# Output projection of a gMLP layer by column halves with four blocks' rows kept, and weight sums on VectorE at longer intervals

## The chip, the cores and the metric

The kernel runs on one core of one Trainium2 chip. The metric is device time of one execution in microseconds (us); the median of several runs counts.

## What is computed

A two-layer decoder trunk on a residual stream x of 2048 rows by 1024 columns, in float32. Layer 0 is a hybrid attention layer (eight heads of dilated sliding-window attention and four heads of differential attention behind one input projection). Layer 1, which is the last stage of the kernel, is a gated MLP:

```python
h = rms_norm(x, norm_g)
u, v, g = split(h @ w_in)                     # 1024 -> 3 x 2048
u = gelu(u)
v = layer_norm(gelu(v), ln_g, ln_b)
sp = einsum('gts,bnsgc->bntgc', tril(w_s), v by chunks of 128 rows, 8 groups) + b_s
y = u * sp * silu(g)
x = x + y @ w_out                             # 2048 -> 1024
```

## The kernel before

Rows are handled in 16 blocks of 128. TensorE (PE) multiplies in a split float32 form: every operand is held as a rounded high part and a low rest, made by `split` (L91): a cast on ScalarE (L92) and a subtraction on VectorE (L93). A product then takes three matmuls: high by high, high by low, low by high.

The order of PE's instructions is the order of the program. The other engines' orders, and those of the DMA queues, come from a planner that simulates the kernel; each queue is then in order. Most loads are issued from the SP queue, most stores from the POOL queue. A tile belongs to a tag with a fixed number of buffers, and a new tile waits for the release of the oldest.

Stage one (0 to about 1420 us) runs eight units. In each, `project` multiplies all 16 blocks by one eighth of the input weights, and between its steps the attention of the unit before is woven in. `quarter_sums` (L282) is woven in too: in 48 pieces it loads parts of the last layer's input weights (L290), takes four differences on GpSimd (POOL, L292 to L295) and stores them (L296) as tensors `t`; `project` calls it once in every block above 8 (L330). It has one buffer, tag tq. Then come `out_first` and `out_second`, the attention's output projections. `out_second` reloads the first half's sums (L766, SP queue), adds, stores x1, squares its rows (L779) and, but for the last two blocks, scales, transposes and stores them as `h2`.

The last stage (from about 1750 us) takes the blocks in four groups of four. Per group it forms `v`, `u` and `g` by Strassen's scheme (seven products, `strassen` L914) in two column rounds (cc 0 and 1). `rows_sums` (L964) loads h2 and makes the seven row operands; their scaling for the last two blocks is left to `turn` (L997), called in the first group. Weights come through `slot` (L861): either a raw load of 512 KB into one of three wr buffers and a split into one of five w2 buffers, or, where `kept` names a copy made earlier, a load of the 1 MB high and low parts from HBM (tensor `ws`). After `g` of a round comes the output projection (L1145 to L1170): for each of two column sets c, four slots with all 1024 output columns are fetched, and for each of the four blocks the rows of y are transposed and split (`turned`, tag yT2, two buffers) and multiplied, 12 matmuls for each half of the output columns, L1161 to L1163:

```python
seq = [(c, b) for c in range(2) for b in blocks]
...
wo2 += slot(wout[:, k0 + k:k0 + k + 1], 1, k0 + k)
```

The first group splits these weights and stores them; groups two to four load the stored form. So there are eight projections, two per group. The mixing in `u` uses another pair of buffers, tag vs.

Of the kernel before, what the change touches and what calls it, by code (L numbers as in the profile page):

```python
# [8 lines left out]
F32 = mybir.dt.float32  # L9
# [8 lines left out]
P = 128  # L18
# [17 lines left out]
DWR, WS, VS_BUFS = 3, 5, 2  # L36
# [24 lines left out]
def _trunk(tc, a, out):  # L61
# [3 lines left out]
    with ExitStack() as top:  # L65
# [25 lines left out]
        def split(hi, lo, src, E=V):  # L91
            A.copy(hi, src)  # L92
            return E.tensor_sub(lo, src, hi.bitcast(F32))  # L93
# [24 lines left out]
        with ExitStack() as st:  # L118
# [161 lines left out]
            def quarter_sums():  # L280


                for m in (1, 0, 2):
                    for kc in range(4):
                        for e in range(0, 1024, 256):
# [6 lines left out]
                            G.tensor_sub(t[:, 0, 0], t[:, 0, 1], t[:, 0, 0])  # L292
                            G.tensor_sub(t[:, 0, 1], t[:, 1, 1], t[:, 0, 1])
                            G.tensor_sub(t[:, 1, 1], t[:, 1, 1], t[:, 0, 0])
                            G.tensor_sub(t[:, 1, 0], t[:, 1, 0], t[:, 1, 1])  # L295
                            G.dma_start(t_s[m][kc][:, :, e:e + 256], t.rearrange("p a b e -> p (a b) e"))  # L296

# [9 lines left out]
            def project(c):  # L307
# [4 lines left out]
                for b in range(NB):  # L312
# [11 lines left out]
                    for dc in range(DC):  # L324
# [5 lines left out]
                        if not first and b > 8 and dc == 1:  # L330
                            next(sums, None)
# [416 lines left out]
            def out_second():  # L748
# [77 lines left out]
        with ExitStack() as st:  # L826
# [17 lines left out]
            for tag, bufs, shape, dt in (  # L844
# [3 lines left out]
                    [("acc", GB, [P, D], F32), ("ln", 2, [P, 2, 512], F32), ("yT2", 2, H, F32R),  # L848
                     ("vs", VS_BUFS, [P, 2, 512], F32R), ("wsp", 1, [P, 2, SG, P], F32R), ("vn", 2, [P, 512], F32),
# [9 lines left out]
            last_load = None  # L859

            def slot(src, n, kept=None):  # L861


                nonlocal last_load
# [4 lines left out]
                else:  # L869
                    raw = tile_([P, 2, 512], F32, "wr", DWR).rearrange("p k e -> p (k e)").rearrange("p (n e) -> p n e", n=n)  # L870
                    last_load = nc.sync.dma_start(raw, src)
                    split(z[:, 0], z[:, 1], raw)
# [90 lines left out]
            def rows_sums(gi, j):  # L963
# [5 lines left out]
                for k in range(2):  # L969
                    nc.sync.dma_start(hr[:, 2 * k:2 * k + 2].rearrange("p q c t -> p (q c t)"), h2_s[b + 2 * k])  # L970
# [4 lines left out]
                def parts(i, src):  # L975
                    split(ht[i][:, 0], ht[i][:, 1], src)
# [20 lines left out]
            def turn(b):  # L997

                with tc.issue_after(urgent.ins):
                    factor(w1, b)  # L1000
                for n in range(2):
                    xr = tile_([P, 512], F32, "ct", 4)
                    nc.sync.dma_start(xr, x1_s[b][:, 512 * n:512 * n + 512])
                    A.activation(xr, xr, AF.Copy, scale=r2[b][:, 0:1])
                    pt = psum("pp", [P, 512], 2).rearrange("p (c t) -> p c t", t=P)
                    for i in range(4):
                        T.transpose(pt[:, i], xr[:, i * P:i * P + P], ident)
# [13 lines left out]
            for gi in range(NG):  # L1021
# [44 lines left out]
                for cc in range(2):  # L1066
# [61 lines left out]
                    def turned(b, c):  # L1128
# [4 lines left out]
                        yT = tile_(H, F32R, "yT2", 2)  # L1133
# [11 lines left out]
                    seq = [(c, b) for c in range(2) for b in blocks]  # L1145
                    for n, (c, b) in enumerate(seq):
                        if n % GB == 0:
                            k0 = columns(cc, c).start // P
                            wo2 = []
                            for k in range(4):  # L1150
                                wo2 += slot(wout[:, k0 + k:k0 + k + 1], 1, k0 + k)
                        yT, nxt = nxt, turned(seq[n + 1][1], seq[n + 1][0]) if n < 7 else None
                        if cc == 0 and c == 0:
# [3 lines left out]
                        for h in range(2):  # L1157
                            es = slice(512 * h, 512 * h + 512)
                            po = psum("y", [P, 512], 3)
                            for i in range(4):  # L1160
# [69 lines left out]
```

## Time and profile before

| what | us |
|---|---|
| median of 3 runs | 3221.08 |
| lowest and highest | 3219.82, 3221.86 |
| the profiled execution | 3229.59 |
| its span | 3227.8 |
| PE busy in the span | 3021.7 (94%) |
| VectorE busy | 2042.0 (63%) |
| ScalarE busy | 1588.7 (49%) |
| GpSimd busy | 859.9 (27%) |

The span runs from the first to the last instruction that the profiler saw; 1.8 us of the profiled execution lie around it. PE busy overstates PE's work, since matmuls overlap in the records: one of 128x512 is recorded with some 0.39 us, while the next one starts 0.23 us after it. PEclk is TensorE's granted clock; 1.00 stands for 2.4 GHz and 0.50 for 1.2 GHz, and a value between is a mean over a stretch.

### The profile page before, as it was taken

The numbers are of one execution on the slowest core, as the hardware profiler recorded it, in microseconds if no ns is written. First come the engines' busy times: TensorE is split into PE (matmuls) and PEld (weight loads), VectorE is DVE, ScalarE is ACT, GpSimd is POOL, SyncE is SP. The second block draws the span as 40 slices with busy tenths as digits, with TensorE's granted clock in tenths as the row PEclk, the third lists the DMA queues.
The fourth block names the chain that finished last, engine by engine and source line by source line (L and its number), as shares of the span: only waits on it lengthen the run. The fifth ranks groups of instructions, "written<-read, shape, count | busy, mean of one in ns | idle before, by whom it ended". The sixth has DMA issues, their size and how long they took to land.

```text
span 3227.8 us, 45405 instructions
## 1 busy us (share of the span) xinstructions
PE 3021.7 (94%) x15240; PEld 2516.7 (78%) x15240; DVE 2042.0 (63%) x4582; ACT 1588.7 (49%) x2964; POOL 859.9 (27%) x2031
## 2 busy tenths in 40 slices
PE   7889999999999998999998899999899999999998
PEld 6678777887888787887886788787787777777787
DVE  5435775467745685467777686858465774758463
ACT  5535655455555555544455564545252553436251
POOL 5537563565536564552121000000000000000000
PEclk9999999999999999999999999999999999999999
DMA  9977967687687967768347776677465764557553
GB/s 346 333 217 242 257 217 217 218 244 224 204 231 228 266 201 218 244 192 238 126 147 265 248 241 254 223 240 242 156 201 202 250 215 150 177 191 245 182 170 143
DMA packets 376074, 710.68 MB, mean 220 GB/s; under 512 B 62113, under 2 KB 176929, under 8 KB 363553
## 3 DMA queue, kind: packets, MB, share of 16 engines
q1 hardware_dynamic: 348640, 603.70, 59.7%
q0 software_dynamic: 27200, 104.09, 8.5%
q8 instruction: 120, 1.97, 0.3%
q14 instruction: 114, 0.93, 0.1%
HBM read 531.25 MB, written 151.26 MB: 211 GB/s over the span
## 4 chain that ended last, share of the span: by engine, by line
PE 72%; DMA 13%; DVE 8%; ACT 3%; issue 2%; SPq 1%; POOL 0%; ACTq 0%; DVEq 0%; POOLq 0%
PE x L926 15%; PE y L926 11%; PE pm L326 5%; PE pm L327 4%; PE pm L328 4%; PE y L1161 4%; PE y L1162 3%; PE y L1163 3%; PE po L645 3%; PE pu L549 3%; DMA w<-ws 3%; PE s_ps L506 3%; DMA hT<-hts 2%; PE sd_ps L608 2%; PE sd_ps L609 2%
## 5 line engine op out<-in xcount | busy, mean ns | idle before, releaser
L926 PE MATMUL x<-w,h 128*128 128x512 f32 x2304 | 557.2, 396 | 15.0 <-ACT w L92 9.4
L93 DVE TENSOR_TENSOR w<-wr,w 128x1024 fp32r<-128x1024 f32 x328 | 399.3, 1220 | 205.1 <-ACT w L92 203.8
L926 PEld LDWEIGHTS x<-w,h 128*128 128x128 f32 x2304 | 433.4, 190 | 115.1 <-ACT w L92 10.5
L326 PE MATMUL pm<-wh,hT 128*128 128x512 f32 x1024 | 452.5, 442 | 53.0 <-DMA hT<-hts 33.3
L92 ACT CAST w<-wr 128x1024 fp32r<-128x1024 f32 x328 | 341.8, 1048 | 239.4 <-PE y L1163 89.6
L926 PE MATMUL y<-w,h 128*128 128x512 f32 x1728 | 414.0, 393 | 0.0
L327 PE MATMUL pm<-wl,hT 128*128 128x512 f32 x1024 | 409.6, 400 | 2.3 <-POOL wl L93 2.3
L328 PE MATMUL pm<-wh,hT 128*128 128x512 f32 x1024 | 410.1, 401 | 0.1
L926 PEld LDWEIGHTS y<-w,h 128*128 128x128 f32 x1728 | 322.9, 188 | 71.9
L326 PEld LDWEIGHTS pm<-wh,hT 128*128 128x128 f32 x1024 | 199.8, 195 | 76.1 <-issue 19.5
L1161 PE MATMUL y<-w,yT 128*128 128x512 f32 x512 | 219.6, 429 | 39.7 <-DMA w<-ws 39.7
L1164 DVE TENSOR_TENSOR acc<-y,acc 128x512 f32<-128x512 f32 x128 | 88.3, 690 | 236.1 <-PE y L1163 236.1
L328 PEld LDWEIGHTS pm<-wh,hT 128*128 128x128 f32 x1024 | 196.5, 192 | 45.8 <-DVE hT L218 0.9
L615 ACT ACTIVATE sd<-sd,nmd 128x128 f32<-128x128 f32 (+15 forms) x128 | 154.0, 1203 | 135.1 <-DVE nmd L611 130.6
L327 PEld LDWEIGHTS pm<-wl,hT 128*128 128x128 f32 x1024 | 199.4, 195 | 20.6 <-POOL wl L93 4.6
L1163 PE MATMUL y<-w,yT 128*128 128x512 f32 x512 | 210.5, 411 | 3.6 <-DVE yT L93 3.6
L1162 PE MATMUL y<-w,yT 128*128 128x512 f32 x512 | 210.6, 411 | 0.2 <-DVE w L93 0.2
L517 ACT ACTIVATE sm<-sm,um 128x256 f32<-128x256 f32 (+1 forms) x256 | 115.6, 486 | 138.0 <-DVE um L515 137.7
L549 PEld LDWEIGHTS pu<-vt,pTs 128*128 128x128 f32 x1200 | 161.5, 193 | 27.3 <-ACT u L552 9.0
L515 DVE CUSTOM_DVE_ANT_0 sm<-s_ps,masks 128x256 f32<-128x256 f32 (+1 forms) x224 | 84.8, 415 | 142.1 <-PE s_ps L506 142.0
L549 PE MATMUL pu<-vt,pTs 128*128 128x65 f32 x1200 | 157.7, 269 | 11.1 <-ACT u L552 7.2
L1161 PEld LDWEIGHTS y<-w,yT 128*128 128x128 f32 x512 | 101.9, 199 | 73.4 <-DMA w<-ws 52.9
(217 smaller groups left out, 5986.5 us busy)
## 6 DMA issues: line engine op xcount, KB each, us to landing
hT<-hts SPq DMA_DIRECT2D x224, 512.0 KB, 4.8
wr<-t SPq DMA_DIRECT2D x168, 512.0 KB, 4.5
wr<-in_sgu_w_in SPq DMA_DIRECT2D x144, 512.0 KB, 4.6
w<-ws SPq DMA_DIRECT2D x72, 1024.0 KB, 6.9
tq<-in_sgu_w_in SPq DMA_DIRECT2D x96, 256.0 KB, 3.4
t<-tq POOLq DMA_DIRECT2D x48, 512.0 KB, 4.7
ws<-w POOLq DMA_DIRECT2D x24, 1024.0 KB, 8.4
hts<-hT SPq DMA_DIRECT2D x32, 512.0 KB, 7.0
```

The source lines that it names most:

```text
L92: A.copy(hi, src)
L93: return E.tensor_sub(lo, src, hi.bitcast(F32))
L326: T.matmul(pm, z[:, 0, k], w[dc][0], start=dc == 0, stop=False)
L327: T.matmul(pm, z[:, 0, k], w[dc][1], start=False, stop=False)
L328: T.matmul(pm, z[:, 1, k], w[dc][0], start=False, stop=dc == DC - 1)
L517: A.activation(sm[:, t, :w], sm[:, t, :w], AF.Exp, bias=nm, scale=-1.0)
L549: T.matmul(pu[:, g0 % 4 + t], pTs[:, t, P * q:P * q + P], vt[pat][:, vb, 65 * i:65 * i + 65], start=q == 0, stop=q == nk - 1)
L615: A.activation(sm[:, :L], sm[:, :L], AF.Exp, bias=nm[:, nch - 1:nch], scale=-1.0, accum_out=lsum)
L926: T.matmul(acc, z[:, p, kc], w[kc][q], start=start and kc == k == 0, stop=kc == 3 and k == 2, skip_group_check=True)
L1161: T.matmul(po, yT[:, 0, i], wo2[i][0][:, es], start=i == 0, stop=False)
L1162: T.matmul(po, yT[:, 0, i], wo2[i][1][:, es], start=False, stop=False)
L1163: T.matmul(po, yT[:, 1, i], wo2[i][0][:, es], start=False, stop=i == 3)
```

## The change

- The output projection takes, for each column set c, first one half of the output columns for all four blocks and then the other. Its weights come in two slots per half (two weight rows by 512 columns each) instead of four per column set, always raw and split, with no copy kept in HBM. The transposed rows of the four blocks are made in the first half and kept for the second. They now share the tag vs, which has four buffers; yT2 is gone.
- `turn` comes after the seventh and eleventh of sixteen steps (before: after the fourth and sixth of eight), loads both halves first and squares the rows itself; `out_second` no longer squares the last two blocks.
- The first group's h2 loads are issued from ScalarE's queue instead of SP, and its row splits are queued behind the latest weight split on ScalarE and VectorE.
- `out_second` loads x1p from the POOL queue instead of SP.
- The weight sums are subtracted on VectorE. Load and subtraction are separate steps, taken in turn from block 4 of a unit on, two steps per 12 of `project`'s steps.

```diff
-DWR, WS, VS_BUFS = 3, 5, 2
+DWR, WS, VS_BUFS = 3, 5, 4
...
         def split(hi, lo, src, E=V):
-            A.copy(hi, src)
-            return E.tensor_sub(lo, src, hi.bitcast(F32))
+            return A.copy(hi, src), E.tensor_sub(lo, src, hi.bitcast(F32))
...
                             yield
-                            G.tensor_sub(t[:, 0, 0], t[:, 0, 1], t[:, 0, 0])
...
+                            V.tensor_sub(t[:, 0, 0], t[:, 0, 1], t[:, 0, 0])
...
                             G.dma_start(t_s[m][kc][:, :, e:e + 256], t.rearrange("p a b e -> p (a b) e"))
+                            yield
...
-                        if not first and b > 8 and dc == 1:
+                        if not first and b > 3 and (8 * b + dc) % 12 in (8, 3):
                             next(sums, None)
...
-                        nc.sync.dma_start(x1[n], x1p_s[b][:, 512 * n:512 * n + 512])
+                        G.dma_start(x1[n], x1p_s[b][:, 512 * n:512 * n + 512])
...
-                    for n in range(2):
-                        sq = w1.tile([P, 512], F32, name="sqx", tag="wr", bufs=WR_BUFS)
-                        A.activation(sq, x1[n], AF.Square, accum_out=r2[b][:, 2 + n:3 + n])
                     if b < NB - LATE:
+                        for n in range(2):
+                            sq = w1.tile([P, 512], F32, name="sqx", tag="wr", bufs=WR_BUFS)
+                            A.activation(sq, x1[n], AF.Square, accum_out=r2[b][:, 2 + n:3 + n])
                         factor(w1, b)
...
-                    nc.sync.dma_start(hr[:, 2 * k:2 * k + 2].rearrange("p q c t -> p (q c t)"), h2_s[b + 2 * k])
+                    (nc.sync if gi else nc.scalar).dma_start(hr[:, 2 * k:2 * k + 2].rearrange("p q c t -> p (q c t)"), h2_s[b + 2 * k])
...
                 def parts(i, src):
-                    split(ht[i][:, 0], ht[i][:, 1], src)
+                    with ExitStack() as behind:
+                        if gi == 0 and halves:
+                            for z in halves:
+                                behind.enter_context(tc.issue_after(z.ins))
+                        split(ht[i][:, 0], ht[i][:, 1], src)
...
             def turn(b):
-                with tc.issue_after(urgent.ins):
-                    factor(w1, b)
+                xr = [tile_([P, 512], F32, "ct", 4) for _ in range(2)]
                 for n in range(2):
-                    xr = tile_([P, 512], F32, "ct", 4)
-                    nc.sync.dma_start(xr, x1_s[b][:, 512 * n:512 * n + 512])
-                    A.activation(xr, xr, AF.Copy, scale=r2[b][:, 0:1])
+                    nc.sync.dma_start(xr[n], x1_s[b][:, 512 * n:512 * n + 512])
+                    sq = tile_([P, 512], F32, "th", 2)
+                    A.activation(sq, xr[n], AF.Square, accum_out=r2[b][:, 2 + n:3 + n])
+                factor(w1, b)
+                for n in range(2):
+                    A.activation(xr[n], xr[n], AF.Copy, scale=r2[b][:, 0:1])
...
-                        yT = tile_(H, F32R, "yT2", 2)
+                        yT = tile_([P, 2, 512], F32R, "vs", VS_BUFS).rearrange("p k (c t) -> p k c t", t=P)
...
-                    seq = [(c, b) for c in range(2) for b in blocks]
-                    for n, (c, b) in enumerate(seq):
+                    seq = [(c, h, b) for c in range(2) for h in range(2) for b in blocks]
+                    yT = {blocks[0]: nxt}
+                    for n, (c, h, b) in enumerate(seq):
+                        es = slice(512 * h, 512 * h + 512)
                         if n % GB == 0:
                             k0 = columns(cc, c).start // P
                             wo2 = []
-                            for k in range(4):
-                                wo2 += slot(wout[:, k0 + k:k0 + k + 1], 1, k0 + k)
-                        yT, nxt = nxt, turned(seq[n + 1][1], seq[n + 1][0]) if n < 7 else None
-                        if cc == 0 and c == 0:
+                            for k in range(0, 4, 2):
+                                wo2 += slot(wout[:, k0 + k:k0 + k + 2, es], 2)
+                        if n + 1 < len(seq) and seq[n + 1][1] == 0:
+                            yT[seq[n + 1][2]] = turned(seq[n + 1][2], seq[n + 1][0])
+                        if cc == 0 and c == h == 0:
                             acc[b] = tile_([P, D], F32, "acc", GB)
...
-                        for h in range(2):
-                            es = slice(512 * h, 512 * h + 512)
-                            po = psum("y", [P, 512], 3)
...
+                        po = psum("y", [P, 512], 3)
+                        for i in range(4):
+                            T.matmul(po, yT[b][:, 0, i], wo2[i][0], start=i == 0, stop=False)
+                            T.matmul(po, yT[b][:, 0, i], wo2[i][1], start=False, stop=False)
+                            T.matmul(po, yT[b][:, 1, i], wo2[i][0], start=False, stop=i == 3)
...
-                        if gi == 0 and cc == 0 and n in (3, 5):
-                            turn(NB - LATE + n // 4)
-                        for _ in range(2):
-                            next(todo, None)
+                        if gi == 0 and cc == 0 and n in (6, 10):
+                            turn(NB - LATE + n // 8)
+                        next(todo, None)
```

## Rows read from the trace of the kernel before

**Rows 1.** The page's chain that ended last, by engine.

```profile
PE 72%; DMA 13%; DVE 8%; ACT 3%; issue 2%; SPq 1%; POOL 0%; ACTq 0%; DVEq 0%; POOLq 0%
```

**Rows 2.** Eight projections: stretch, us, five engines' busy time, PEclk, DMA, GB/s.

```profile
1930.21:1982.08 51.87, 49.61 (x236) 40.25 (x234) 26.99 (x37) 13.65 (x19) 2.67 (x5) 1.00 0.62 245
2066.25:2119.13 52.88, 48.40 (x220) 38.19 (x218) 35.92 (x53) 16.98 (x26) 2.66 (x5) 1.00 0.72 275
2285.94:2345.42 59.48, 51.39 (x219) 40.18 (x218) 18.35 (x26) 7.28 (x11) 0.00 (x0) 0.94 0.25 99
2429.57:2486.90 57.33, 50.81 (x219) 39.61 (x218) 28.07 (x43) 11.38 (x18) 0.00 (x0) 0.94 0.45 170
2650.50:2711.63 61.13, 53.81 (x219) 41.76 (x218) 18.35 (x26) 7.28 (x11) 0.00 (x0) 0.89 0.25 96
2795.78:2857.32 61.54, 53.68 (x219) 41.73 (x218) 27.98 (x43) 11.39 (x18) 0.00 (x0) 0.89 0.37 141
3022.67:3083.62 60.95, 53.96 (x220) 41.99 (x218) 18.36 (x26) 7.30 (x11) 0.00 (x0) 0.89 0.25 95
3167.77:3223.70 55.93, 50.74 (x219) 39.68 (x217) 16.40 (x24) 4.45 (x8) 0.00 (x0) 0.94 0.32 125
```

**Rows 3.** PE, third projection: start, us, what, [idle before <-releaser].

```profile
2285.94 0.47 PE L1161 MATMUL y<-w,yT 128*128 128x512 f32 x1
...
2289.22 0.50 PE L1161 MATMUL y<-w,yT 128*128 128x512 f32 x1 [1.64 <-DMA w<-ws]
...
2321.53 0.79 PE L1161 MATMUL y<-w,yT 128*128 128x512 f32 x1 [1.55 <-DMA w<-ws]
...
2345.42 1.79 PE L926 MATMUL x<-w,h 128*128 128x512 f32 x7
```

**Rows 4.** The page's groups of instructions, output projection and weight split.

```profile
L1161 PE MATMUL y<-w,yT 128*128 128x512 f32 x512 | 219.6, 429 | 39.7 <-DMA w<-ws 39.7
...
L93 DVE TENSOR_TENSOR w<-wr,w 128x1024 fp32r<-128x1024 f32 x328 | 399.3, 1220 | 205.1 <-ACT w L92 203.8
...
L92 ACT CAST w<-wr 128x1024 fp32r<-128x1024 f32 x328 | 341.8, 1048 | 239.4 <-PE y L1163 89.6
```

**Rows 5.** The chain in order of time: start, us, what (two windows of it).

```profile
2240.88 11.11 PE x L926 x48
...
2295.59 0.44 PE pp L1132 x4
...
2322.33 0.43 PE y L1162
```

**Rows 6.** The page's DMA issues: count, KB, median us to landing.

```profile
wr<-in_sgu_w_in SPq DMA_DIRECT2D x144, 512.0 KB, 4.6
...
w<-ws SPq DMA_DIRECT2D x72, 1024.0 KB, 6.9
```

**Rows 7.** PE in order of time, second projection: its longest wait.

```profile
2076.65 0.63 PE L1132 MATMUL pp<-ident,vv 128*128 128x128 f32 x4 [2.98 <-DVE vv L1126]
```

**Rows 8.** Start of the last stage, in order of time: PE, ScalarE, VectorE.

```profile
1741.01 0.63 ACT L779 ACTIVATE sqx<-x 128x512 f32<-128x512 f32 x1 [2.07 <-DVE x L731]
...
1750.42 0.79 PE L926 MATMUL x<-w,h 128*128 128x512 f32 x1 [9.37 <-ACT w L92]
1753.98 7.35 PE L926 MATMUL x<-w,h 128*128 128x512 f32 x23 [2.77 <-DVE w L93]
...
1744.28 1.29 DVE L93 TENSOR_TENSOR h<-hr,h 128x512 fp32r<-128x512 f32 x2
```

**Rows 9.** Waits (us, times, longest) and one group of lines.

```profile
POOL tq L292 <- DMA tq<-in_sgu_w_in: 105.5, 36, 7.6
...
SPq L290 <- DMA t<-tq: 177.2, 40, 9.2
...
PE pm L326 <- DMA hT<-hts: 10.8, 7, 4.6
...
L509 DVE TENSOR_TENSOR sm<-s_ps,masks 128x256 f32<-128x256 f32 x80 | 33.8, 423 | 103.6 <-PE s_ps L506 103.4
```

More of the change, by code (lines that the diff above doesn't have):

```diff
@@ L291, in quarter_sums @@
                             yield
-                            G.tensor_sub(t[:, 0, 0], t[:, 0, 1], t[:, 0, 0])
-                            G.tensor_sub(t[:, 0, 1], t[:, 1, 1], t[:, 0, 1])
-                            G.tensor_sub(t[:, 1, 1], t[:, 1, 1], t[:, 0, 0])
-                            G.tensor_sub(t[:, 1, 0], t[:, 1, 0], t[:, 1, 1])
+                            V.tensor_sub(t[:, 0, 0], t[:, 0, 1], t[:, 0, 0])
+                            V.tensor_sub(t[:, 0, 1], t[:, 1, 1], t[:, 0, 1])
+                            V.tensor_sub(t[:, 1, 1], t[:, 1, 1], t[:, 0, 0])
+                            V.tensor_sub(t[:, 1, 0], t[:, 1, 0], t[:, 1, 1])
                             G.dma_start(t_s[m][kc][:, :, e:e + 256], t.rearrange("p a b e -> p (a b) e"))
+                            yield
             sums, loaded = quarter_sums(), []
@@ L847, in _trunk @@
                     [(f"vv{i}", 1, [P, SW], F32) for i in range(3)] +
-                    [("acc", GB, [P, D], F32), ("ln", 2, [P, 2, 512], F32), ("yT2", 2, H, F32R),
-                     ("vs", VS_BUFS, [P, 2, 512], F32R), ("wsp", 1, [P, 2, SG, P], F32R), ("vn", 2, [P, 512], F32),
+                    [("acc", GB, [P, D], F32), ("ln", 2, [P, 2, 512], F32), ("vs", VS_BUFS, [P, 2, 512], F32R), ("wsp", 1, [P, 2, SG, P], F32R), ("vn", 2, [P, 512], F32),
                      ("th", 2, [P, 512], F32), ("u2", 2, [P, 512], F32), ("st6", GB, [P, 4, 6], F32)] +
@@ L857, in _trunk @@
                 ahead_ps[tag] = psum(tag, [P, 512], bufs)
-            last_load = None
+            last_load, halves = None, None
             def slot(src, n, kept=None):
-                nonlocal last_load
+                nonlocal last_load, halves
                 flat = tile_([P, 2, 1024], F32R, "w2", WS)
@@ L871, in slot @@
                     last_load = nc.sync.dma_start(raw, src)
-                    split(z[:, 0], z[:, 1], raw)
+                    halves = split(z[:, 0], z[:, 1], raw)
                     if kept is not None:
@@ L1156, in _trunk @@
                                 nc.sync.dma_start(acc[b], x1_s[b])
-                        for h in range(2):
-                            es = slice(512 * h, 512 * h + 512)
-                            po = psum("y", [P, 512], 3)
-                            for i in range(4):
-                                T.matmul(po, yT[:, 0, i], wo2[i][0][:, es], start=i == 0, stop=False)
-                                T.matmul(po, yT[:, 0, i], wo2[i][1][:, es], start=False, stop=False)
-                                T.matmul(po, yT[:, 1, i], wo2[i][0][:, es], start=False, stop=i == 3)
-                            V.tensor_add(acc[b][:, es], po, acc[b][:, es])
-                            if cc == 1 and c == 1:
-                                nc.sync.dma_start(out[b * P:(b + 1) * P, es], acc[b][:, es])
-                        if gi == 0 and cc == 0 and n in (3, 5):
-                            turn(NB - LATE + n // 4)
-                        for _ in range(2):
-                            next(todo, None)
+                        po = psum("y", [P, 512], 3)
[3 more added lines that the diff above has]
+                            T.matmul(po, yT[b][:, 1, i], wo2[i][0], start=False, stop=i == 3)
+                        V.tensor_add(acc[b][:, es], po, acc[b][:, es])
+                        if cc == 1 and c == 1:
+                            nc.sync.dma_start(out[b * P:(b + 1) * P, es], acc[b][:, es])
+                        if gi == 0 and cc == 0 and n in (6, 10):
+                            turn(NB - LATE + n // 8)
+                        next(todo, None)
 def _host_constants():
```

2 lines of the change are left out of this document (1 added, 1 removed).

## The prediction

> **What bounds the kernel now.** I read the chain that ended last first: PE carries 72% of it, DMA 13%, VectorE 8%, GpSimd nothing [rows 1]. So time is won where PE stands still, and work that leaves GpSimd is worth nothing by itself. Next comes the table of the eight output projections, each from its first matmul to the first matmul of what follows (the last one to its end) [rows 2]. The reader is to see that they hold the same matmuls and yet last 51.9 and 52.9 us in group one and 55.9 to 61.5 in groups two to four, where the granted clock is 0.89 or 0.94 instead of 1.00. PE in order of time says why: in the third projection it stops over and over for a load of stored weights, here 1.64 and 1.55 us [rows 3]; over all projections the first matmul of each triple waited 39.7 us for such loads [rows 4]. Behind such a stop matmuls follow each other at 0.43 us instead of 0.23 [rows 5]: the lower of the two clock levels, 1.2 instead of 2.4 GHz. Group one, which loads raw weights and splits them, has no such waits.
>
> What a projection has to cost: 48 matmuls take 11.11 us, 0.2315 each, and four transposes 0.44 us [rows 5]. A projection has 192 matmuls and, inside the stretch, seven such sets of transposes: 44.4 + 3.1 = 47.5 us. The six stored ones sum to 356.4 us [rows 2], so 356.4 - 6 x 47.5 = 71.4 us are lost in them.
>
> **Output projection: what goes.** Before, a column set holds four of the five w2 buffers until its last block is done, so the next four 1 MB loads, 6.9 us each at the median [rows 6], can hardly start before they are wanted. After, a half holds two, and the next two fit into the other three. Each half lasts 4 x 12 x 0.2315 = 11.1 us and needs two raw loads of 512 KB, 4.6 us each for the raw loads of the same row length [rows 6], so 9.2 us even one after the other, and three wr buffers let them overlap. No wait for w<-ws can be left there.
>
> **What comes.** Groups two to four split what they loaded ready-made: 3 x 16 slots more, each 1.05 us on ScalarE and 1.22 on VectorE [rows 4]. That is 50 and 59 us, 8.4 and 9.8 per projection. In these projections VectorE is busy 16 to 28 us of 56 to 62, ScalarE 4 to 11 [rows 2]; 38 of 48 us is the most that results. The splits lie beside PE's matmuls as they do in group one. If that cover were gone, the whole 59 us would stand on the path.
>
> A second cost is the shorter time for transposed rows. In a first half a block now lasts 12 x 0.2315 + 0.44 = 3.2 us, before 6.0. In it the next rows must be transposed, cast and subtracted, while VectorE adds one result and does half a split. By the 128x1024 row, a 128x512 operation is some 0.6 to 0.7 us there and 0.5 to 0.6 on ScalarE: two of them, one of ScalarE and half a split make about 2.5 us per block, under 3.2 but not by much. The second half makes no rows and has slack.
>
> Group one bounds what is left. Its second projection, with splits and the next group's row splits on VectorE, lost 52.9 - 47.5 = 5.4 us, 2.98 of them in one wait for VectorE [rows 2, 7]. I give the second projections of groups two and three this 5.4. Its first lost 51.9 - 47.5 = 4.4, of which 4 x 0.44 = 1.8 are the transposes of two `turn` calls; that leaves 2.6 as the bound for the other four, which have no row splits, and I take 1. Left over: 2 x 5.4 + 4 x 1 = 15; gain 71.4 - 15 = **57 us**, bounds 39 (5.4 in all six) and 71. Group one itself keeps its time: the copies it no longer stores left on the POOL queue.
>
> `turn` now also squares rows and makes the factor, between the seventh and eleventh step; its loads go out early on SP and PE meets its transposes some 19 us into the projection or later. Nothing. The final store hangs on the last addition as before.
>
> Here the Trainium skill speaks against the change: "DMA: Bandwidth & Descriptors", section "Bandwidth", asks for transfers of at least 1 MiB and gives smaller ones a lower rate. The rows agree on the rate: 4.6 us for 512 KB is worse than 6.9 for 1 MB [rows 6]. But the raw load carries the same weights in half the bytes, so by the rows it is 2.3 us shorter per slot; by the page's rule alone the loads would bind, which is a rival below.
>
> **Start of the last stage.** PE stops at 1750.42 - 9.37 = 1741.05 and runs freely from 1753.98 [rows 8]: 12.9 us, one matmul inside. ScalarE's queue is held by the squares of the last block (it waited 2.07 us for VectorE ahead of them), then it casts row parts ahead of the first weights, and VectorE begins the row parts only at 1744.28 [rows 8]. After the change the squares and factors of the last two blocks are gone, weight splits go ahead of row parts, and SP no longer holds the first weight loads behind x1p loads that wait for buffers. Then the first matmul needs one cast and one subtraction, 1.05 + 1.22 = 2.3 us [rows 4], at worst after PE has stopped: gap 0 to 2.3, gain 10.4 to 12.7. But row parts that VectorE made in the gap now compete with the first seven products: 14 splits at 1.22, 14 row parts and 8 sums at 0.65, 6 Strassen sums and 8 statistics at 0.65 make 40.5 us against 168 x 0.2315 = 39 for PE, so some 2 us come back. I take **8 us**, bounds 3 (only the second wait, 2.77, goes) and 12.7. The new wait, an h2 load on ScalarE's queue, would hold casts behind it; the rows were stored long before, so it is short. x1p loads on POOL stand in front of stores that nobody awaits at that time.
>
> **Weight sums.** SP waited 177.2 us at the loads of these sums for the store before, with the loads of hT queued behind; only 10.8 us of PE's waits were for hT between 200 and 1420 us [rows 9]. That much could be won. VectorE gets 192 subtractions of 128x256: no row shows one from SBUF; a quarter of 1.22 us is 0.31, and the same size from PSUM takes 0.42 [rows 4, 9], so 59 to 81 us, in bursts of 1.2 to 1.7. Behind the first of a burst, which waits for its load, stand the softmax reductions and PE behind these. GpSimd waited 105.5 us for such loads [rows 9], partly because SP issued them late. If 6% of it reaches PE, as of SP's wait (10.8 of 177.2), it costs 6 us. Against a part of 10.8 I take **0**, bounds 11 won and 6 lost; what is beyond is a rival. More vs buffers in `u`: nothing.
>
> **Sum.** 57 + 8 + 0 = 65 us. The profiled execution took 3229.6 us, 8.5 above the median of the runs (0.26%). 3229.6 - 65 = 3164.6, less 8.5: **3156 us** as a median. All low bounds together: 39 + 3 - 6 = 36, 3185; all high: 71 + 12.7 + 11 = 95, 3126.
>
> **Rivals.** (a) VectorE becomes the limit of the projections: rows late in the first halves, 5.4 us left in each, and the start of the stage wins only 3. That is the 3185 corner, about 3179 with the sums at 0. For it: 2.5 us of work in 3.2, and the wait of 2.98 us in group one. Against: ScalarE and VectorE mostly idle in groups two to four. (b) Everything is hidden, second projections too, since only two slots instead of four are split at their start, and hT waits go: 71 + 10 + 8 = 89 gained, 3132. (c) Loads bind: raw loads take the 6.9 us of the larger ones and come one by one, so a half of 11.1 us waits for 13.8. That is 2.7 x 32 halves = 86 us back, against 65 gained: 3242, slower. It turns the sign once a load takes over 6.6 us with nothing beside it (2 x 6.6 - 11.1 = 2.1, times 32); group one, without any such wait on the same weights, speaks against it. It is where the rule of the Trainium skill's page "DMA: Bandwidth & Descriptors" would lead. (d) The sums hold VectorE: if all 105.5 us of waits for their loads pass through VectorE to PE, 3156 + 105 = 3261, slower; it decides once two thirds of them do. Against: loads now have some seven steps of `project` until the subtraction and SP is not held by the store.
>
> **How the numbers follow.** Forecast 0.60, (a) 0.19, (b) 0.12, (c) 0.03, (d) 0.04, and 0.02 that gains and new waits cancel. About 0.2%, 6.4 us, is what a measurement of this kernel can tell from no change. So faster 0.91, same 0.02, slower 0.07. The range takes in the bounds of the terms, (a) and most of (b): 3130 to 3185.
>
> **What would show it.** Right: in the profile after, w<-ws loads fall from 72 to 24 and weight splits rise from 328 to 376; the projections of groups two to four last 48 to 53 us at clock 1.00; PE's gap at the start of the last stage is under 4 us; GpSimd's busy time falls by some 150 us and the span hardly notices. Wrong: PE waits for yT or w from VectorE in first halves (a), waits for wr loads (c), or VectorE idle ahead of the subtractions with PE's softmax waits grown between 200 and 1200 us (d).

## The result

| | median of runs, us | lowest and highest | ratio to before, 95% interval |
|---|---|---|---|
| before | 3220.45 | 3213.70, 3221.86 | 1 |
| after | 3185.82 | 3182.00, 3193.26 | 0.9899 [0.9875, 0.9924] |

The change gains 35 us, 1.0%. The sign was forecast, the size was not: 65 us were expected, and 3185.8 lies 0.8 us outside the range. The profiled execution of after took 3193.26 us (span 3191.5), 36.3 less than that of before.

### The profile after

The page, part 1, busy time by engine, and its group of weight splits on VectorE:

```profile
PE 3001.6 (94%) x15240; PEld 2508.5 (79%) x15240; DVE 2142.9 (67%) x4822; ACT 1641.5 (51%) x3012; POOL 726.6 (23%) x1855
...
L92 DVE TENSOR_TENSOR w<-wr,w 128x1024 fp32r<-128x1024 f32 x376 | 459.3, 1222 | 240.2 <-ACT w L92 239.3
```

The page's DMA issues, the raw loads that are new and the line that answers to [rows 6]:

```profile
wr<-in_sgu_w_out SPq DMA_DIRECT2D x64, 512.0 KB, 3.9
...
w<-ws SPq DMA_DIRECT2D x24, 1024.0 KB, 5.8
```

So the change does what it says: 48 splits more (376 for 328), 48 loads of stored weights fewer (24 for 72), GpSimd 133 us less busy.

The eight projections, columns as in [rows 2] (stretch, length, busy time of PE, PEld, VectorE, ScalarE, GpSimd, PEclk, DMA share, GB/s):

```profile
1933.32:1983.82 50.50, 49.64 (x236) 40.13 (x235) 36.72 (x73) 19.78 (x31) 0.00 (x0) 1.00 0.36 115
2067.99:2128.41 60.42, 50.28 (x220) 39.46 (x219) 37.88 (x55) 18.36 (x27) 0.00 (x0) 0.94 0.42 139
2292.29:2340.25 47.96, 47.59 (x220) 38.56 (x218) 31.50 (x43) 14.52 (x19) 0.00 (x0) 1.00 0.29 89
2424.41:2484.24 59.83, 50.92 (x219) 40.07 (x218) 37.87 (x55) 18.36 (x27) 0.00 (x0) 0.94 0.42 141
2650.13:2698.10 47.97, 47.61 (x219) 38.57 (x218) 31.50 (x43) 14.53 (x19) 0.00 (x0) 1.00 0.29 89
2782.26:2841.78 59.52, 50.77 (x219) 40.47 (x218) 37.85 (x55) 18.44 (x27) 0.00 (x0) 0.94 0.39 124
3007.45:3055.42 47.97, 47.61 (x220) 38.57 (x219) 31.51 (x43) 14.53 (x19) 0.00 (x0) 1.00 0.29 90
3139.57:3187.54 47.97, 47.61 (x219) 38.38 (x217) 22.50 (x31) 8.57 (x12) 0.00 (x0) 1.00 0.17 61
```

The reader is to see two kinds of lines. Four stand at 47.96 or 47.97 us with clock 1.00, half a microsecond above the ideal of 47.5. Three, the second projections of groups one to three, stand at 59.5 to 60.4 with clock 0.94. The eight sum to 422.1 us, before 461.1 [rows 2]: 39 us gained in all. What the three have and the others have not is the making of the next group's row operands (`rows_sums`). What PE waits for from the first projection to the end says the same (us in total, times, longest):

```profile
PE pp L1137 <- DVE vv L1131: 17.3, 3, 5.8
PE y L1170 <- DVE vs L92: 11.7, 12, 1.7
```

Waits for stored or raw weights, 39.7 us before [rows 4], are gone, and three waits of 5.8 us for VectorE have come. They are one and the same place, four transposes early in the second projection, where before had 2.98 us in group one [rows 7]; and behind them a matmul starts 0.43 us after the one before instead of 0.23 for a while, at a granted clock of 0.50 (2434.80 to 2438.00 us in group two), the lower of the two clock levels:

```profile
2078.40 1.09 PE L1137 MATMUL pp<-ident,vv 128*128 128x128 f32 x4 [5.77 <-DVE vv L1131]
2079.14 0.78 PE L1168 MATMUL y<-w,vs 128*128 128x512 f32 x1
2079.71 0.63 PE L1169 MATMUL y<-w,vs 128*128 128x512 f32 x1
2080.14 0.63 PE L1170 MATMUL y<-w,vs 128*128 128x512 f32 x1
```

In group two the 12.3 us above 47.5 are, by PE's rows there, 5.8 for this wait, some 2.5 for the lower clock behind it (12 matmuls and four transposes in 5.7 us instead of 3.2) and 3.1 for two waits at L1170, for the low part of the transposed rows; the rest is small.

VectorE in order of time, in the 15 us ahead of that place in group two (start, us, what):

```profile
2419.77 0.68 DVE L986 TENSOR_TENSOR ct<-hr 128x512 f32<-128x512 f32 x1
2420.37 0.69 DVE L1130 SCALAR_TENSOR_TENSOR th<-th,ct 128x512 f32<-128x512 f32 x1
2420.97 1.22 DVE L92 TENSOR_TENSOR w<-wr,w 128x1024 fp32r<-128x1024 f32 x1
2422.10 0.69 DVE L987 TENSOR_TENSOR ct<-ct,hr 128x512 f32<-128x512 f32 x1
2422.70 0.69 DVE L992 TENSOR_TENSOR hr<-hr 128x512 f32<-128x512 f32 x1
2423.31 0.69 DVE L1130 SCALAR_TENSOR_TENSOR th<-th,ct 128x512 f32<-128x512 f32 x1
...
2432.18 0.70 DVE L92 TENSOR_TENSOR h<-hr,h 128x512 fp32r<-128x512 f32 x1
2432.78 0.69 DVE L1171 TENSOR_TENSOR acc<-y,acc 128x512 f32<-128x512 f32 x1
2433.38 0.69 DVE L1130 SCALAR_TENSOR_TENSOR th<-th,x 128x512 f32<-128x512 f32 x1
2433.98 1.30 DVE L1131 TENSOR_TENSOR vv<-vv,th 128x512 f32<-128x512 f32 x2
```

No line has an idle time in brackets: the queue runs without a gap. Of the 23 operations that start in it (the window below counts one more, begun just before) nine belong to the next group's rows (L986, L987, L992, L995 and five splits into h, 0.60 us from one start to the next, 5.4 us) and three are weight splits (1.14 each, 3.4 us); the products that PE waits for (L1130, L1131) stand between and behind them. The same as numbers, windows of 15 us, of after and then of before (group one, group two):

```profile
2063.35:2078.40 15.05, 7.94 (x38) 5.93 (x37) 15.05 (x24) 7.52 (x12) 0.00 (x0) 0.89 0.47 146
2419.77:2434.82 15.05, 7.95 (x38) 5.93 (x37) 15.05 (x24) 7.51 (x12) 0.00 (x0) 0.95 0.45 145
```

```profile
2061.65:2076.65 15.00, 10.68 (x50) 8.14 (x49) 15.00 (x24) 7.41 (x12) 1.86 (x4) 1.00 1.02 394
2425.00:2440.05 15.05, 13.29 (x64) 10.29 (x62) 12.14 (x21) 6.09 (x12) 0.00 (x0) 1.00 0.86 334
```

VectorE, third busy number, is full in both windows of after and in group one of before, not in group two of before. That is my theory for the missing gain, called "order": VectorE isn't too slow for a projection (38 of 60 us busy), it is full for 15 us, and work that nobody needs yet stands in those 15 us ahead of work that PE needs at once.

### The profile page after: what moved, and what is told of

Its sections match the earlier page's. It is cut to its first block, busy times and chain, and to the rows that moved or that the text cites. A ratio compares the mean times of both kernels' runs of the same rounds, so it can differ in the third digit from the quotient of the medians.

```text
span 3191.5 us, 45535 instructions
## 1 busy us (share of the span) xinstructions
PE 3001.6 (94%) x15240; PEld 2508.5 (79%) x15240; DVE 2142.9 (67%) x4822; ACT 1641.5 (51%) x3012; POOL 726.6 (23%) x1855
## 4 chain that ended last, share of the span: by engine, by line
PE 72%; DMA 11%; DVE 9%; issue 3%; ACT 3%; POOL 1%; SPq 1%; DVEq 0%; ACTq 0%; POOLq 0%
PE x L925 14%; PE y L925 11%; PE pm L326 5%; PE pm L328 5%; PE pm L327 5%; PE pu L549 3%; PE y L1170 3%; PE y L1168 3%; PE y L1169 3%; PE po L645 3%; PE s_ps L506 3%; DMA hT<-hts 2%; DMA tq<-in_sgu_w_in 2%; PE pT L525 2%; PE sd_ps L608 1%
## 5 line engine op out<-in xcount | busy, mean ns | idle before, releaser
L92 DVE TENSOR_TENSOR w<-wr,w 128x1024 fp32r<-128x1024 f32 x376 | 459.3, 1222 | 240.2 <-ACT w L92 239.3
L92 ACT CAST w<-wr 128x1024 fp32r<-128x1024 f32 x376 | 394.2, 1049 | 235.1 <-PE y L1170 89.8
L1170 PE MATMUL y<-w,vs 128*128 128x512 f32 x512 | 205.6, 401 | 11.8 <-DVE vs L92 11.7
L1168 PE MATMUL y<-w,vs 128*128 128x512 f32 x512 | 209.7, 409 | 0.5 <-ACT vs L92 0.5
L1169 PE MATMUL y<-w,vs 128*128 128x512 f32 x512 | 204.3, 399 | 0.0
L645 PEld LDWEIGHTS po<-vd,pTds 128*128 128x128 f32 x1088 | 145.9, 192 | 15.0 <-ACT pTds L653 1.6
```

What stands on the lines that cost most here:

```text
L92: return A.copy(hi, src), E.tensor_sub(lo, src, hi.bitcast(F32))
L645: T.matmul(po, pTs[:, k], v[:, k4 + k], start=k4 + k == 0, stop=k4 + k == i)
L1168: T.matmul(po, yT[b][:, 0, i], wo2[i][0], start=i == 0, stop=False)
L1169: T.matmul(po, yT[b][:, 0, i], wo2[i][1], start=False, stop=False)
L1170: T.matmul(po, yT[b][:, 1, i], wo2[i][0], start=False, stop=i == 3)
```

## Experiments

Ratios are to the kernel before, run beside each kernel on the same chip. Its median there was 3231.1 us for the first four kernels below, 3215.1 for the next four and 3224.6 for the last two, so ratios are compared, not times. Line numbers are those of each run's own kernel and shift by a few from run to run.

### Row parts held back

The kernel after, with the sums and splits of the next group's rows queued behind the fourth addition of the second projection, and called only from the fifth step on.

```diff
@@ rows_sums
+    if gi:
+        behind.enter_context(tc.issue_after(half_done.ins))
@@ projection
-    V.tensor_add(acc[b][:, es], po, acc[b][:, es])
+    added = V.tensor_add(acc[b][:, es], po, acc[b][:, es])
+    if n == 3:
+        half_done = added
...
-    next(todo, None)
+    if n > 3:
+        next(todo, None)
+        if n in (5, 7):
+            next(todo, None)
```

> The changed kernel with one edit: the next group's row parts (rows_sums) are made in steps 5 to 16 of a group's second output projection instead of from step 1 on, and on VectorE they are queued behind the addition of the fourth step. No work is added or left out. Theory 'order' (in the second projections of groups one to three VectorE runs the next group's row parts ahead of the last gating products and of the transposed rows that PE needs next): the three waits of 5.8 us for vv vanish, these projections fall from 59.5 to 60.4 us to 48 to 51, and the kernel takes 3186 - 27 to 36 = 3150 to 3159 us. Rival 'load' (the weight splits leave VectorE too little time, whatever its order): the same work is still there, the projections stay above 57 us, 3180 to 3190 us. Rival 'spacing' (3.2 us per block are too short for the transposed rows): the waits of 1.3 to 1.7 us for the rows' low part stay in every first half, and at most 17 us go.

Measured 3151.8 us (3150.3 to 3153.5), ratio 0.9751 [0.9732, 0.9770]. Its second projections of groups one and two, and PE's waits from the first projection on:

```profile
2062.80:2111.39 48.59, 47.86 (x219) 38.46 (x217) 38.17 (x57) 19.19 (x27) 0.00 (x0) 1.00 0.50 169
...
2408.16:2456.84 48.68, 47.95 (x220) 38.37 (x217) 38.18 (x57) 19.20 (x27) 0.00 (x0) 1.00 0.51 169
```

```profile
PE pp L1101 <- DVE vs L92: 5.0, 3, 1.7
PE y L1175 <- DVE vs L92: 4.0, 11, 0.4
```

VectorE does the same work there (38.2 us busy, 37.9 in after), the 5.8-us waits are gone, the clock stays at 1.00, and a second projection takes 48.6 us instead of 60. The eight sum to 388.6 us, 72.5 less than before. So the mechanism is shown: at the same amount of VectorE's work, its place in the queue decides. The rival "load" falls with that, and so does "spacing": the waits for the low part of the rows (L1170 in after, L1175 here) came down from 11.7 to 4.0 us, 0.4 at the longest. The other line, 5.0 us, is the mixing in `u`; it had 5.2 in before and in after too. The edit also puts off the h2 loads and ScalarE's casts of the row parts, but among PE's waits in the projections of after there is none for a load, and only 0.5 us for ScalarE. This kernel is faster than both. The expected 3150 to 3159 us were reckoned from another chip's 3186, so that 3151.8 lies among them is in part luck: by ratio the gain over after is 1.5%, some 48 us, of which 33.5 lie in the projections; what the rest is was not taken apart.

### The projection alone, the start alone

The first is the kernel before with the change's projection loop and vs buffers only. The second is the kernel before with only the start of the last stage (h2 loads, splits behind weights, `turn`).

```diff
-    DWR, WS, VS_BUFS = 3, 5, 2
+    DWR, WS, VS_BUFS = 3, 5, 4
-    yT = tile_(H, F32R, "yT2", 2)
+    yT = tile_([P, 2, 512], F32R, "vs", VS_BUFS).rearrange("p k (c t) -> p k c t", t=P)
-    seq = [(c, b) for c in range(2) for b in blocks]
...
+    seq = [(c, h, b) for c in range(2) for h in range(2) for b in blocks]
...
```

> The kernel before with the projection change alone (column halves, four blocks' rows kept in the vs buffers, raw weights split in every group, turn after steps 7 and 11). If the parts add up: the eight projections take 422 us together instead of 461, second projections near 60, first ones 48, and the kernel takes 3221 - 39 = 3182 us (3178 to 3186). If the start of the last stage or the sums interact with it: outside 3174 to 3190.

Measured 3192.2 us, ratio 0.9873 [0.9854, 0.9893]: as much as the whole change. Its eight projections sum to 426.0 us, 35 less than before, and the pattern is that of after: 48.0 us in the first projections of groups two to four, 60.2, 61.0 and 60.6 in the second ones of groups one to three.

> The kernel before with the change at the start of the last stage alone (x1p loads from the POOL queue, squares of the last two blocks moved into turn, first h2 loads from ScalarE's queue, row parts behind the weight splits; sums and projection as before). If the parts add up: the gap of PE between the last transposes and free running shrinks by 6 us, 3221 - 6 = 3215 us (3211 to 3218). If the forecast's 8 us was right and something else ate it in the changed kernel: 3211 to 3214. If squares and factors in turn now hold PE in the first projection: above 3218.

Measured 3233.2 us, ratio 0.9995 [0.9976, 1.0014]: nothing. The gain at the start is there (181.9 us from PE's arrival in the last stage to the first projection, 189.2 in before) and goes again at the first projection, where the heavier `turn` now stands on the path. PE's waits in the first projection:

```profile
PE pp L1012 <- ACT ct L1009: 5.0, 1, 5.0
PE pp L1137 <- DVE th L1014: 1.8, 1, 1.8
```

`turn` in this kernel is still called after the fourth and sixth step; the transposes of the second call wait 5.0 us for rows that ScalarE scales, and ScalarE for the factor, which now comes only from here. The projection lasts 58.5 us instead of 51.9 [rows 2]. In after it lasts 50.5.

### The weight sums of before

The kernel after, with the subtractions back on GpSimd, one step in every block above 8, and the second yield of a round gone.

```diff
-    V.tensor_sub(t[:, 0, 0], t[:, 0, 1], t[:, 0, 0])
+    G.tensor_sub(t[:, 0, 0], t[:, 0, 1], t[:, 0, 0])
...
-    if not first and b > 3 and (8 * b + dc) % 12 in (8, 3):
+    if not first and b > 8 and dc == 1:
```

> The changed kernel with the weight sums put back as before: on GpSimd, one whole step per block from block 9 on. Theory 'sums cost' (PE reaches the end of the attention stages 8.6 us later than before because of the sums): the last stage begins at 1738 to 1740 us instead of 1747, hT waits of PE between 200 and 1420 us fall from 23.7 to about 11 us, and the kernel takes 3174 to 3180 us. Rival 'noise of one execution': the last stage begins at 1745 to 1749 us all the same, 3183 to 3189 us.

Measured 3193.9 us, ratio 0.9880 [0.9860, 0.9901]; after has 0.9899 [0.9875, 0.9924]. The intervals overlap; no difference in time is shown. The signs of the theory "sums cost" came, or nearly, in this profile: PE reaches the last stage at 1740.96 us (after: 1749.37), and its waits for hT between 200 and 1420 us are 9.9 us (after: 23.7). But the eight projections take 428.0 us here, 6 more than in after, and the span is only 3.6 us shorter. Why the projections are longer was not taken apart.

### Weights of the halves stored by group one

The kernel after, but groups two to four load split copies of the halves' weights, 1 MB each, as before did with whole rows.

```diff
-    wo2 += slot(wout[:, k0 + k:k0 + k + 2, es], 2)
+    wo2 += slot(wout[:, k0 + k:k0 + k + 2, es], 2, (k0 + k, h))
```

> The kernel after, but groups two to four load the split copies of the halves' weights that group one stored (1 MB each), as the kernel before did with whole rows, instead of splitting raw loads again. It asks how much of the 5.8 us wait at the second projections of groups two and three is the splits' and how much the row parts'. Theory 'order' (row parts stand ahead of critical work in VectorE's queue; three splits of 1.14 us stand there too): the wait of PE for the product L1131 falls from 5.8 to about 2.4 us in groups two and three and stays 5.8 in group one, second projections of groups two and three 60 to about 55, time about 10 us less, ratio to before 0.985 to 0.988. Rival 'splits are the cause': the wait goes entirely, those projections near 49, ratio 0.982. Rival 'the stored loads were the trouble, whatever their spacing': waits for w<-ws come back in the projections of groups two to four, 1 to 2 us at a time, with half clock behind them; ratio above 0.992.

Measured 3166.2 us (3154.7 to 3169.1), ratio 0.9837 [0.9803, 0.9872]. The projections of group two (the second one of group three lasts 50.2 us):

```profile
2287.77:2335.12 47.35, 47.35 (x220) 38.62 (x218) 25.43 (x36) 10.39 (x15) 0.00 (x0) 1.00 0.42 148
2419.28:2469.02 49.74, 47.95 (x220) 38.36 (x217) 29.56 (x45) 12.72 (x19) 0.00 (x0) 1.00 0.62 218
```

The rival "splits are the cause" came nearest: the 5.8-us wait went entirely in groups two and three (it stays in group one, which still splits), not only by the 3.4 us that three splits take. And no wait for w<-ws came back, though the loads are as large and as many as before. Both causes are needed: row parts without splits fit into VectorE's 15 us (13.9 of 15.0 us busy ahead of the same transposes in group two, which wait for nothing), splits without row parts fit too, as with the row parts held back; both together don't. That the wait went by more than the 3.4 us may be the order again: the planner queues anew for each kernel, and here one more of the gating products (L1130) stands ahead of the row parts. No run separates the two. That also says what the halves did by themselves: taking two slots instead of four at a time removed the waits for loads, whichever form was loaded; splitting raw weights again in groups two to four was not needed for it, and cost some 10 us in each of two projections, as long as the row parts were not held back.

Group one's first projection pays here: it lasts 57.1 us for 50.5 in after, with a wait of 4.1 us behind `turn`'s factor (L111); its second lasts 56.6 for 60.4. What the stores have to do with that was not taken apart.

### Weight sums, three ways, on the kernel with row parts held back

The first has the sums as before the change, the second the subtractions on GpSimd at the new intervals, the third the subtractions on VectorE from block 9 on, two steps a block (shown here).

```diff
-    if not first and b > 3 and (8 * b + dc) % 12 in (8, 3):
+    if not first and b > 8 and dc in (1, 5):
```

> The kernel with the next group's row parts held back, with the weight sums as before the change (GpSimd, one step a block from block 9 on). Theory 'VectorE': sums on VectorE delay the softmax; this one is 5 to 10 us faster than the kernel with row parts held back (3144 if that is 3152). Theory 'loads': the new interval draws the sums' loads into blocks 4 to 8, where the DMA engines are full; this one is 5 to 10 us faster too. Theory 'nothing' (stage one ends at the same time within the spread of single profiles, 0 to 10 us): within 0.2% of it.

> The kernel with the next group's row parts held back, with the subtractions of the weight sums on GpSimd but at the new intervals. Theory 'VectorE': as fast as with the sums of before, 5 to 10 us under the kernel with row parts held back. Theory 'loads': no faster than the kernel with row parts held back, and PE is late by 12 to 16 us for a while about 450 and 1190 us, as there. Theory 'nothing': within 0.2%.

> The kernel with the next group's row parts held back, with the weight sums on VectorE from block 9 on, two steps a block, so that none falls into blocks 4 to 8. Theory 'VectorE': no faster than the kernel with row parts held back (3152). Theory 'loads': 5 to 10 us faster, and the lateness about 450 and 1190 us is gone. Theory 'nothing': within 0.2%.

| sums | ratio to before, 95% interval |
|---|---|
| as in after (row parts held back) | 0.9751 [0.9732, 0.9770] |
| as before the change | 0.9766 [0.9741, 0.9790] |
| GpSimd, new intervals | 0.9774 [0.9749, 0.9800] |
| VectorE, late | 0.9777 [0.9752, 0.9802] |

All four agree within 0.3%, and their intervals overlap. The theory "nothing" had put the three within 0.2% of the first, and two lie just beyond, on the slower side; both rivals asked for a kernel that is 5 to 10 us faster, and none is. So "nothing" comes nearest. The lateness of PE with the sums as in after is seen in the profiles, but passing. In the profile after, PE is 12.7 us later than in before at its 2,000th matmul (453 us) and 13.9 at its 6,000th (1197 us), and in the three other kernels with these sums (row parts held back, halves stored, row parts on GpSimd) it is so again, by 12 to 20; 400 matmuls later 2 to 10 us are left. With the subtractions on GpSimd at the new intervals PE is 7.6 and 5.9 us later at these two places, so the theory "loads", which asked for 12 to 16 there, has no support.

### Row parts on GpSimd

The kernel after, with the sums and subtractions of the row parts of groups two to four on GpSimd, which has nothing to do then.

```diff
-    split(ht[i][:, 0], ht[i][:, 1], src)
+    split(ht[i][:, 0], ht[i][:, 1], src, E=G if gi else V)
...
-    V.tensor_add(s1, a21, a22)
+    E.tensor_add(s1, a21, a22)
```

> The kernel after, with VectorE's half of the next group's row parts (the sums and the subtractions of the splits, groups two to four) on GpSimd, which is idle in the last stage; order and splits of weights stay. Theory 'VectorE's time in the fifteen us ahead of the second projection': 9 of its operations of 0.6 us leave the queue ahead of the products that PE waits for, the waits of 5.8 us go in all three, second projections fall from 60 to about 49, time as with the row parts held back, ratio to before 0.974 to 0.979. Rival 'the two engines hold each other up': VectorE's 128x512 operations, 0.68 us in the kernel after, get longer while GpSimd works, and the second projections stay above 55, ratio 0.984 or more. Rival 'only the weight splits matter': the second projections stay at 57 to 60.

Measured 3182.9 us, ratio 0.9872 [0.9828, 0.9916]: hardly anything, although VectorE has nine operations less in its queue. The second projections last 57.4, 55.7 and 57.0 us. The waits of 5.8 us are gone (3.1 us in total are left, in three waits), but those for the low part of the rows have grown to 15.1 us, 3.7 at the longest, from 11.7 and 1.7 in after. VectorE in order of time in group two, then GpSimd beside it:

```profile
2417.16 1.18 DVE L1131 SCALAR_TENSOR_TENSOR th<-th,ct 128x512 f32<-128x512 f32 x1
2418.26 2.32 DVE L92 TENSOR_TENSOR w<-wr,w 128x1024 fp32r<-128x1024 f32 x1
2420.51 1.75 DVE L1132 TENSOR_TENSOR vv<-vv,th 128x512 f32<-128x512 f32 x1
2422.18 1.75 DVE L1131 SCALAR_TENSOR_TENSOR th<-th,ct 128x512 f32<-128x512 f32 x1
2423.85 0.68 DVE L92 TENSOR_TENSOR vs<-pp,vs 128x512 fp32r<-128x512 f32 x1
```

```profile
2417.74 1.76 POOL L92 TENSOR_TENSOR h<-ct,h 128x512 fp32r<-128x512 f32 x1
...
2421.67 1.71 POOL L92 TENSOR_TENSOR h<-hr,h 128x512 fp32r<-128x512 f32 x1
```

A product of 128x512 that takes 0.69 us in after takes up to 1.75 here, about as long as one GpSimd operation beside it, and a weight split up to 2.32 instead of 1.22; the subtraction whose source is in PSUM (vs<-pp) still takes 0.68. So the rival "the two engines hold each other up" is shown, and the gain of the shorter queue is given back.

### Row parts held back in the kernel before

The first experiment's edit on the kernel before; the row parts wait for the second block's last addition.

```diff
+    if n == 1 and h == 1:
+        half_done = added
...
-    for _ in range(2):
+    for _ in range(3 if n > 1 else 0):
         next(todo, None)
```

> The kernel before, with the next group's row parts held back to the third block of the second projections, as was done to the kernel after. Theory 'it is the change that uses up VectorE's slack': in the kernel before a block has 6 us instead of 3, so little is to be had: the second projection of group one falls from 52.9 to 49 to 51, those of groups two and three stay at 55 to 61 because they wait for stored weights, ratio 0.996 to 1.000. Rival 'the row parts cost as much in the kernel before': 5 us or more in each of the three, ratio under 0.995.

Measured 3220.1 us, ratio 0.9991 [0.9966, 1.0016]. Its second projections of groups one and two:

```profile
2058.64:2106.72 48.08, 47.92 (x220) 38.40 (x219) 36.76 (x55) 17.83 (x26) 2.67 (x5) 1.00 0.77 303
2413.32:2474.49 61.17, 53.56 (x219) 41.59 (x218) 31.04 (x48) 13.79 (x22) 0.00 (x0) 0.89 0.42 160
```

In group one the 5.4 us that the second projection lost go almost entirely (48.1 us for 52.9); in groups two and three the second projections get no shorter (61.2 and 61.5 us, 57.3 and 61.5 in before); there PE waits 7.6 and 8.1 us for loads of stored weights. So row parts had cost 5 us once in the kernel before; the change made it 12 us three times.

## Why the prediction was partly wrong, point by point

**What bounds the kernel; loads of stored weights.** Right. The 39.7 us of waits [rows 4] are gone, and the four projections without row parts came down to 48.0 us at clock 1.00. I had left 1 us in each of them and 2.6 as the bound; 0.5 is left.

**Left over in the second projections: the step that failed.** I gave 5.4 us to those of groups two and three and let group one keep its 52.9. Measured over 47.5: 12.9, 12.3 and 12.0 us. Against the forecast that is 7.5 + 6.9 + 6.6 = 21 us too much; the other projections gave some 3 us back, so the projections gained 39 us instead of 57. Of the 29 us that the profiled execution is short of the 65 forecast, that is 18; 3 are missing at the start of the last stage, and 8 are PE's later arrival there (below). The mistake has two parts. I took the busy share of VectorE over the whole projection (16 to 28 of 56 to 62 us, 38 of 48 at most) as the cover for the splits, when the 15 us at its start decide; there VectorE was already full in group one of before. And my count of a block's work, 2.5 us in 3.2, had the transposed rows, the addition and half a split, but not the products of L1130 and L1131, which the last of the Strassen products leave over, nor the row parts. Group one was read as a bound for the others while the change halved the time that its blocks have, so it was no bound, not even for itself. The rows of before would have given the size: there the transposes start 2076.65 - 2066.25 = 10.4 us after the projection's first matmul [rows 2, 7], and in after it is 10.4 again in all three groups (2078.40 - 2067.99 in group one). VectorE delivers at the same moment; PE asks for it 12 matmuls, 12 x 0.2315 = 2.8 us, sooner, and 2.98 + 2.8 is the 5.8 measured.

**Splits at no cost.** Right for all projections but those three, wrong there: with row parts behind them they cost the whole margin, as the stored copies show. My rival (a), at 3179 us with a chance of 0.19, named VectorE as the limit and is nearest to the result; it put 5.4 us into every projection and not 12 into three, and the late rows of y that it feared (L1170) are the smaller part of these 12.

**Start of the last stage.** 5 us instead of 8. From PE's arrival to its first projection before took 1930.21 - 1741.05 = 189.2 us [rows 2, 8], after 1933.32 - 1749.37 = 184.0. The first matmul comes at once, as forecast, but the next ones stop for weights and rows, 5.9 us in all (12.1 in before), where I had put the gap under 4:

```profile
1749.37 0.47 PE L925 MATMUL x<-w,h 128*128 128x512 f32 x1
1751.85 1.80 PE L925 MATMUL x<-w,h 128*128 128x512 f32 x5 [2.01 <-DVE w L92]
1755.70 0.80 PE L925 MATMUL x<-w,h 128*128 128x512 f32 x1 [2.05 <-ACT w L92]
...
1761.70 1.66 PE L925 MATMUL x<-w,h 128*128 128x512 f32 x6 [1.39 <-DVE h L92]
```

ScalarE, from the first cast of weights on:

```profile
1743.57 1.05 ACT L92 CAST w<-wr 128x1024 fp32r<-128x1024 f32 x1 [0.91 <-issue]
1746.91 0.62 ACT L92 CAST h<-hr 128x512 fp32r<-128x512 f32 x1 [2.29 <-DMA hr<-h]
1754.60 1.04 ACT L92 CAST w<-wr 128x1024 fp32r<-128x1024 f32 x1 [7.07 <-DMA x<-x]
```

I had counted on splits going on ahead of the stage. One does; the second cast waits 7.07 us for a DMA of x tiles. I read that as memory of a w2 buffer that the stage before still holds until its last rows are stored; no experiment shows it. And alone the new start was worth nothing by time.

**`turn`: nothing.** Right in after, where the first projection lasts 50.5 us; the start alone shows that it isn't free everywhere (5.0 us).

**Weight sums: nothing.** Right by time. The waits did not go as I had argued: SP's wait for the store fell, PE's for hT rose (us in total, times, longest; between 200 and 1420 us for PE):

```profile
SPq L289 <- DMA t<-tq: 38.3, 19, 4.6
...
PE pm L326 <- DMA hT<-hts: 23.7, 7, 6.1
```

177.2 and 10.8 us before [rows 9]. In this profile PE comes to the last stage 8.3 us later than in before (1749.37 against 1741.05), and with 39.0 gained in the projections and 5.2 at the start that makes the 36 us of the profiled executions. But the kernel with stored halves, with the same sums, arrives at 1741.07, and the start alone, with the old sums, at 1751.36. So 8 us are within the spread between single profiles, and the four kernels above agree by time; a cost of a few us is not excluded by that.

**Rivals.** (b) fell: the second projections weren't hidden; with the row parts held back, though, the eight projections gain 72.5 us, where it had put 71 for six. (c) fell: raw loads of 512 KB took 3.9 us and no wait for them is among PE's. The rule of the Trainium skill ("DMA: Bandwidth & Descriptors", section "Bandwidth") on larger transfers decided nothing here: with 1 MB copies of the halves no wait for weights was found either. (d) fell with the sums.

## What to carry to other kernels

When work is moved onto an engine that is half idle, don't compare its busy share over the stage: open the ten or twenty microseconds ahead of the place where the critical engine will next want something from it, and list what stands in its queue there. If that stretch is full, hold back what nobody needs yet before anything else is tuned; here that was worth more than the whole change (1.5% beside 1.0%), and without the change it was worth nothing by time. And when a wait for another engine is read off a profile, ask when that engine delivers, not how long the wait is: here, in group one, delivery stayed at 10.4 us and the wait doubled because PE came sooner. When a change has two parts that go together (here halves and raw weights), try each: only one of them was needed.

## What the hardware showed

With the row parts on GpSimd, VectorE's operations with both sources in SBUF took up to 1.75 us instead of 0.69 (128x512) and up to 2.32 instead of 1.22 (128x1024) while GpSimd ran operations of 1.7 us, and those with one source in PSUM kept their 0.68. GpSimd's operations of 128x512 grew as well: 1.29 us while VectorE read PSUM or stood still, 1.7 to 2.3 beside two-tile operations. The Trainium skill, "SBUF — State Buffer", section "Who interferes with whom", says that a VectorE instruction with two SBUF inputs contends with a GpSimd instruction that reads SBUF, and that the port pair which the two engines share is an exclusive lock. The trace agrees on the contention by these numbers; whether one engine is blocked for the whole of the other's instruction they don't settle, since VectorE's operation grew by 1.06 us and GpSimd's takes 1.29 undisturbed. In this kernel an idle GpSimd was therefore no place for work that is meant to relieve VectorE in a stretch where VectorE reads two tiles from SBUF (ratio 0.9872 for 0.9899).
